# An expert layer's elementwise work taken off GpSimd, and its gathers and u tiles moved ahead of the long loop

## The chip, the cores and the metric

The kernel runs on one core of a Trainium2 chip. A core has a matrix engine (PE, with its weight loads shown as PEld), a vector engine (DVE), a scalar engine (ACT), a general engine (GpSimd, shown as POOL) and a queue engine that issues transfers (SP). Sixteen DMA engines move data between the core's memory and HBM. Every engine has its own queue and works through it in order; semaphores make it wait for others. The metric is the device time of one execution in microseconds, the median of several.

## The reference

A decoder trunk over 512 tokens of width 1024: one recurrent layer, then one attention layer, each followed by a PEER expert layer. The change touches the expert layers alone:

```python
def peer(h, w_q, sub_keys, u_tab, v_tab):
    q = (h @ w_q).reshape(B, S, PEER_HEADS, 2, PEER_HALF)          # 8 heads, 2 halves of 128
    s = jnp.einsum('bshpd,hpnd->bshpn', q, sub_keys)               # 128 keys per half
    v1, i1 = lax.top_k(s[..., 0, :], PEER_TOPK)                    # 16 best of each half
    v2, i2 = lax.top_k(s[..., 1, :], PEER_TOPK)
    cand = (v1[..., :, None] + v2[..., None, :]).reshape(B, S, PEER_HEADS, 256)
    cv, ci = lax.top_k(cand, PEER_TOPK)                            # 16 best sums
    e1 = jnp.take_along_axis(i1, ci // PEER_TOPK, axis=-1)
    e2 = jnp.take_along_axis(i2, ci % PEER_TOPK, axis=-1)
    idx = e1 * N_KEYS + e2                                         # 128 experts per token, of 16384
    g = jax.nn.softmax(cv, axis=-1)
    # per token: sum over its 128 experts of g * gelu(h . u_tab[idx]) * v_tab[idx]
```

## The kernel before

The 512 tokens are four blocks of 128. For three of them ("dense" blocks, 384 tokens) the kernel computes all 16384 experts: per tile of 128 experts it multiplies a tile of u (1024 x 128) with the hidden states, applies gelu, multiplies by a gate that is zero for experts not chosen, and multiplies with a tile of v. The fourth block gathers just its own 128 expert rows of u and of v per token by indirect DMA, 256 rows of 128 x 4 KB per layer, and DVE forms dot products (L1104) and weighted sums (L1109).

Each fp32 matrix is split into a rounded high part (ACT, `whi` or `vh`) and a rest (`wlo` or `vl`, a subtraction of 128 x 1024 at L161); a product is three matmuls (L185 to L187). A u tile (`u_part`) is thus a transfer of 512 KB, a copy, a subtraction, 24 matmuls of 384 columns and a gelu; a v tile has 18 matmuls of 512 columns. Weight buffers come in rings of three (`whi`, `wlo`) behind a ring of four raw buffers.

An expert layer goes through three stages:

- Scoring, four groups of two heads. Per group: four query tiles (`pq`, 24 matmuls of 512 columns each), scores (`sc`), top-k per block and half (L729 to L733), candidate sums on GpSimd (`candidates`), their top-k, some conditioning columns of other layers (`ada`, five a group in layer 0 and two in layer 1), and `UPQ[grp]` u tiles that keep PE busy.
- Gate. `decode` turns the top-k results of each block into expert numbers and weights; `gate_prep` transposes them. Then 24 groups of 16 tokens (`gate_group`): one-hot rows of both expert numbers (`o1`, `o2`), the first one weighted by the high and the low part of the gate (`pr[0]`, `pr[1]`), and 32 matmuls that make the tokens' gates over all experts (`wps`), stored to memory (`stg`, `wscr`, 1 MB a group). u tiles run between the groups. Block 3, the gathered one, is decoded last.
- The loop over 128 v tiles. `LEAD` u tiles are done before it (49: 8 in x, 9 in a ring of 12, 32 spilled to memory in `gscr`, 192 KB each, and read back); the other 79 run inside it, one per v tile. The gathers run here too: `goal` spreads 256 of them over the tiles by the weights `wts`.

The order on each engine is set by a scheduler from the program's order, with priorities and `issue_after` ties. In scoring and gate the u tiles' subtractions and the query tiles' are on GpSimd (`eng=nc.gpsimd`, or `wtile`'s default), as is `pr[1]` of every second half group:

```python
(nc.gpsimd if t0 else nc.vector).tensor_tensor(pr[1], o1, toks(gp[:, 1, :]), op=OP.mult)
```

## Time and profile before

| | us |
|---|---|
| median of 3 runs | 3215.36 (3213.15 to 3219.0) |
| profiled execution, its own time | 3213.07 |
| its span, first to last instruction | 3211.2 |
| mean granted clock of TensorE | 0.967 |

The profiled execution lies 2.3 us below the median, and 1.9 us of it lie around the span. Busy time is the time in which an engine executes; idle time counts only where something waits for that engine. "x" counts instructions.

### The profile page before, as it was taken

The numbers are of one execution on the slowest core, as the hardware profiler recorded it, in microseconds if no ns is written. First come the engines' busy times: TensorE is split into PE (matmuls) and PEld (weight loads), VectorE is DVE, ScalarE is ACT, GpSimd is POOL, SyncE is SP. The second block draws the span as 40 slices with busy tenths as digits, with TensorE's granted clock in tenths as the row PEclk, the third lists the DMA queues.
The fourth block names the chain that finished last, engine by engine and source line by source line (L and its number), as shares of the span: only waits on it lengthen the run. The fifth ranks groups of instructions, "written<-read, shape, count | busy, mean of one in ns | idle before, by whom it ended". The sixth has DMA issues, their size and how long they took to land. (4 is left out here: it accounts for less than half of the span.)

```text
span 3211.2 us, 43091 instructions
## 1 busy us (share of the span) xinstructions
PE 3023.7 (94%) x15334; PEld 2646.2 (82%) x15334; DVE 2631.5 (82%) x4865; ACT 1381.3 (43%) x1960; POOL 1338.0 (42%) x907
## 2 busy tenths in 40 slices
PE   6999888889999999999889989888999999999997
PEld 5658878878899999998667768888988999999996
DVE  8859999977788888888768959999766888888887
ACT  5532256643333333333456642466533333333333
POOL 0014555630244444444246625556500444444441
PEclk9999989889999999999889999999999999999999
DMA  7444445589899999999313234355698999999994
GB/s 287 147 155 154 152 152 195 178 284 319 302 355 336 346 342 332 339 335 338 117 37 101 92 128 129 113 192 182 233 311 258 339 337 331 337 334 350 337 332 161
DMA packets 319767, 786.52 MB, mean 245 GB/s; under 512 B 30784, under 2 KB 153792, under 8 KB 313152
## 3 DMA queue, kind: packets, MB, share of 16 engines
q1 hardware_dynamic: 226960, 443.61, 41.7%
q0 software_dynamic: 73728, 268.47, 23.2%
q10 hardware_dynamic: 18864, 71.69, 5.7%
q8 instruction: 121, 1.98, 0.3%
q14 instruction: 94, 0.77, 0.1%
HBM read 713.68 MB, written 69.99 MB: 244 GB/s over the span
## 5 line engine op out<-in xcount | busy, mean ns | idle before, releaser
L185 PE MATMUL u<-hh,wlo 128*128 128x384 f32 x2048 | 700.4, 342 | 10.1 <-ACT gact L896 9.7
L187 PE MATMUL u<-hh,whi 128*128 128x384 f32 x2048 | 698.8, 341 | 0.0
L186 PE MATMUL u<-hl,whi 128*128 128x384 f32 x2048 | 698.0, 341 | 0.0
L1100 POOL DMA_INDIRECT grow<-in_u_dram,idx x256 | 335.1, 1309 | 675.2 <-DVE gdot L1104 533.8
L186 PE MATMUL acc<-vl,ah 128*128 128x512 f32 x1536 | 600.8, 391 | 2.5 <-DVE vl L161 2.5
L161 POOL TENSOR_TENSOR wlo<-raw,whi 128x1024 fp32r<-128x1024 f32 (+2 forms) x183 | 401.3, 2198 | 483.4 <-ACT whi L160 470.8
L187 PE MATMUL acc<-vh,ah 128*128 128x512 f32 x1536 | 600.8, 391 | 0.0
L185 PE MATMUL acc<-vh,al 128*128 128x512 f32 x1536 | 592.1, 389 | 2.2 <-DVE al L161 2.2
L1100 POOL DMA_INDIRECT grow<-in_v_dram,idx x256 | 336.4, 1314 | 374.8 <-DVE gacc L1109 255.7
L161 DVE TENSOR_TENSOR vl<-vraw,vh 128x1024 fp32r<-128x1024 f32 x256 | 313.6, 1225 | 208.8 <-ACT vh L160 198.1
L160 ACT ACTIVATE whi<-raw 128x1024 fp32r<-128x1024 f32 (+2 forms) x364 | 350.2, 963 | 196.5 <-PE acc L187 57.8
L185 PEld LDWEIGHTS u<-hh,wlo 128*128 128x128 f32 x2048 | 393.3, 192 | 17.9 <-issue 10.2
L186 PEld LDWEIGHTS u<-hl,whi 128*128 128x128 f32 x2048 | 393.5, 192 | 6.2
L187 PEld LDWEIGHTS u<-hh,whi 128*128 128x128 f32 x2048 | 393.3, 192 | 0.0
L186 PEld LDWEIGHTS acc<-vl,ah 128*128 128x128 f32 x1536 | 288.2, 188 | 60.7 <-DVE vl L161 3.0
L187 PEld LDWEIGHTS acc<-vh,ah 128*128 128x128 f32 x1536 | 288.2, 188 | 60.3
L185 PEld LDWEIGHTS acc<-vh,al 128*128 128x128 f32 x1536 | 288.4, 188 | 59.4 <-DVE al L161 2.0
L1109 DVE SCALAR_TENSOR_TENSOR gacc<-grow,gdot,gacc 128x1024 f32<-128x1024 f32 x254 | 325.2, 1280 | 13.4 <-DMA grow<-in_v_dram,idx 12.2
L1104 DVE CUSTOM_DVE_ANT_0 grow<-grow,hn 128x1024 f32<-128x1024 f32 x256 | 308.8, 1221 | 19.0 <-DMA grow<-in_u_dram,idx 18.6
L160 ACT ACTIVATE ah<-gact 128x384 fp32r<-128x384 f32 x240 | 125.7, 524 | 438.5 <-DVE gact L985 299.1
L160 ACT ACTIVATE vh<-vraw 128x1024 fp32r<-128x1024 f32 x256 | 268.7, 1051 | 40.5 <-issue 17.7
L896 ACT ACTIVATE gact<-u 128x384 f32<-128x384 f32 x176 | 86.5, 491 | 458.4 <-PE u L187 455.0
(339 smaller groups left out, 4817.1 us busy)
## 6 DMA issues: line engine op xcount, KB each, us to landing
raw<-in_uT_dram SPq DMA_DIRECT2D x256, 512.0 KB
vraw<-in_v_dram SPq DMA_DIRECT2D x256, 512.0 KB
ada_raw<-in_adaw_dram SPq DMA_DIRECT2D x112, 512.0 KB
wscr<-stg ACTq DMA_DIRECT2D x48, 1024.0 KB
wt<-wscr SPq DMA_DIRECT2D x32, 1536.0 KB
raw<-in_w_pq_dram SPq DMA_DIRECT2D x32, 512.0 KB
gscr<-gsp ACTq DMA_DIRECT2D x64, 192.0 KB
gact<-gscr SPq DMA_DIRECT2D x64, 192.0 KB
```

What stands on the lines that cost most here:

```text
L160: nc.scalar.activation(hi, src, AF.Copy)
L161: return (eng or nc.vector).tensor_tensor(lo, src, hi.bitcast(F32), op=OP.subtract)
L185: nc.tensor.matmul(out, al, bh, start=first, stop=False)
L186: nc.tensor.matmul(out, ah, bl, start=False, stop=False)
L187: return nc.tensor.matmul(out, ah, bh, start=False, stop=last)
L896: nc.scalar.activation(gact[t], out[:, :ND], AF.Gelu)
L1100: nc.gpsimd.indirect_dma_start(out=row, out_offset=None, in_=tabs[s], in_offset=bass.IndirectOffsetOnAxis(ap=idx[:, k:k + 1], axis=0))
L1104: nc.vector.tensor_tensor_reduce(row, row, hn, op0=OP.mult, op1=OP.add, scale=1.0, scalar=0.0, accum_out=col)
L1109: nc.vector.scalar_tensor_tensor(acc, row, col, acc, op0=OP.mult, op1=OP.add)
```

## The change

All elementwise work of the expert layers leaves GpSimd for DVE. The gate's one-hot operations are merged in pairs (2048 elements instead of 1024), with the expert numbers and gates laid out by groups of eight tokens for it. The gathered block is scored first in each group, and decoded right after its scores in the last group, so its gathers can start in the gate stage: 12 steps by the end of the u tiles ahead of it, 100 by the end of the gate groups. `LEAD` rises from 49 to 93 u tiles, 76 of them spilled; 23 instead of 10 run in scoring, and those of the gate stage are tied behind the gate group two back (`after=wlast[-2]`). The weights that spread the other 156 gathers over the loop are new, and the first gates have a buffer of their own.

```diff
-SPILL = 32
+SPILL = 76
 LEAD = KC + RING - 3 + SPILL
-UPQ = (1, 2, 3, 4)
-UDEC = 6
-UEND = 3
+UPQ = (5, 6, 6, 6)
+UDEC = 9
+UEND = 5
+FIRST = 12
+EARLY = 100
...
-        nc.gpsimd.tensor_tensor(ca, v4[:, :, 0, 0:4].unsqueeze(3).to_broadcast([P, n, 4, 16]),
+        nc.vector.tensor_tensor(ca, v4[:, :, 0, 0:4].unsqueeze(3).to_broadcast([P, n, 4, 16]),
...
-            o2 = pool.tile(shp, F16, name="o2", bufs=2)
-            o1 = pool.tile(shp, F16, name="o1", bufs=2)
-            pr = [pool.tile(shp, F16, name=f"pr{q}", bufs=2) for q in range(2)]
-            nc.vector.tensor_tensor(o1, io, toks(et[:, 0, :]), op=OP.is_equal)
-            (nc.gpsimd if t0 else nc.vector).tensor_tensor(pr[1], o1, toks(gp[:, 1, :]), op=OP.mult)
-            nc.vector.tensor_tensor(o2, io, toks(et[:, 1, :]), op=OP.is_equal)
-            nc.vector.tensor_tensor(pr[0], o1, toks(gp[:, 0, :]), op=OP.mult)
+            oo = pool.tile(shp, F16, name="oo", bufs=2)
+            pr = pool.tile(shp, F16, name="pr", bufs=2)
+            nc.vector.tensor_tensor(oo, io, toks(et), op=OP.is_equal)
+            two = [P, 2, n4, P, 4]
+            nc.vector.tensor_tensor(pr.rearrange("p (q a) e t -> p q a e t", q=2), oo[:, 0:n4].unsqueeze(1).to_broadcast(two),
+                                    toks(gp).rearrange("p (q a) e t -> p q a e t", q=2), op=OP.mult)
...
-            def u_part(eng=None, after=None):
+            def u_part(after=None):
...
-                hi, lo = self.wtile(io["uT"][l][t], KC, eng=eng or nc.vector)
+                hi, lo = self.wtile(io["uT"][l][t], KC, eng=nc.vector)
...
-                            self.lin(outs[m], self.wtile(io["w_pq"][wq + m], KC), h)
+                            self.lin(outs[m], self.wtile(io["w_pq"][wq + m], KC, eng=nc.vector), h)
...
-                    for b in range(NB):
+                    for b in (nd, *range(nd)):
...
+                        if grp == 3 and b == nd:
+                            for _ in decodes((nd,)):
+                                pass
+                            gsteps = self.gather_steps(gpool, l, *gsel[0], hn)
...
                     for _ in range(UPQ[grp]):
-                        u_part(nc.gpsimd)
+                        u_part()
...
+                steps = decodes(range(nd))
+                for i in range(UDEC):
+                    u_part()
+                    while done < FIRST * (i + 1) // UDEC:
+                        next(gsteps)
+                        done += 1
...
                 for i in range(nt):
                     while state["u"] < n0 + (LEAD - UEND - n0) * (i + 1) // nt:
-                        u_part(nc.gpsimd)
-                    wlast = self.gate_group(pool, l, i // nsg, i % nsg, *prep[i // nsg])
+                        u_part(after=wlast[-2])
+                    wlast.append(self.gate_group(pool, l, i // nsg, i % nsg, *prep[i // nsg]))
...
+                    while done < min(EARLY, FIRST + (EARLY - FIRST) * (i + 1) // (nt - 2)):
+                        next(gsteps)
+                        done += 1
...
-            wts = [0.1 if t < KC + SPILL else 1.0 if t < tail else 0.5 if t < P - 2 else 0.0 for t in range(P)]
+            wts = [0.2 if t < KC else 0.6 if t < KC + SPILL else 2.6 if t < tail else 1.0 if t < P - 2 else 0.0 for t in range(P)]
```

First place: DVE in the gate stage of layer 0. Before, some ten rows between two gate tiles hold gate operations of 1024, decoding (`oh`, `rc`) and position tables (`ps_`):

```order
L834 TENSOR_TENSOR pr_4525<-o_4524,gp 128x1024
L832 TENSOR_TENSOR pr_4526<-o_4524,gp 128x1024
L833 TENSOR_TENSOR o_4523<-iota_e,et 128x1024
L798 TENSOR_TENSOR e_4589<-oh 128x64
L470 TENSOR_SCALAR ps_a<-ps_a,cst 128x512
L834 TENSOR_TENSOR pr_4553<-o_4552,gp 128x1024
L833 TENSOR_TENSOR o_4551<-iota_e,et 128x1024
L831 TENSOR_TENSOR o_4660<-iota_e,et 128x1024
L789 TENSOR_TENSOR oh<-iota_m,rc 128x1024
```

After, the same place on DVE:

```order
L835 TENSOR_TENSOR oo<-iota_e,et 128x2048
L163 TENSOR_TENSOR wlo<-raw,whi 128x1024
L798 TENSOR_TENSOR oh<-oh 128x4x64
L837 TENSOR_TENSOR pr<-oo,gp 128x2048
L1122 SCALAR_TENSOR_TENSOR gacc<-grow,gdot,gacc 128x1024
L837 TENSOR_TENSOR pr<-oo,gp 128x2048
L163 TENSOR_TENSOR wlo<-raw,whi 128x1024
L798 TENSOR_TENSOR oh<-oh 128x4x32
L1122 SCALAR_TENSOR_TENSOR gacc<-grow,gdot,gacc 128x1024
L163 TENSOR_TENSOR wlo<-raw,whi 128x1024
```

Gate operations have doubled in width and halved in number; u subtractions (`wlo`) and weighted sums of gathered rows (`gacc`) now stand between them.

Second place: DVE at the end of a scoring group of layer 0, where `ada_junk` is a conditioning column and `MAX` of `sc` begins the next group's top-k. Before:

```order
L752 MAX_INDEX ci_1544<-cv_1540,c_2146 128x8
L149 ISA ada_junk,mod<-ada_raw,csil,vecs 128x1024
L149 ISA mod 128x1
L752 MAX_INDEX ci_1544<-cv_1540,c_2152 128x8
L149 ISA ada_junk,mod<-ada_raw,csil,vecs 128x1024
L149 ISA mod 128x1
L729 MAX v_1362<-sc 128x8
```

After:

```order
L163 TENSOR_TENSOR wlo<-raw,whi 128x1024
L754 MAX_INDEX ci_1543<-cv_1539,c_2277 128x8
L754 MAX_INDEX ci_1543<-cv_1539,c_2283 128x8
L151 ISA ada_junk,mod<-ada_raw,csil,vecs 128x1024
L151 ISA mod 128x1
L151 ISA ada_junk,mod<-ada_raw,csil,vecs 128x1024
L151 ISA mod 128x1
L163 TENSOR_TENSOR wlo<-raw,whi 128x1024 x2
L731 MAX v_1365<-sc 128x8
```

The splits of the query and u tiles that PE needs for and after the next scores now stand behind this group's top-k and columns.

Third place: GpSimd in the last part of layer 0's gate stage. Before:

```order
L161 TENSOR_TENSOR wlo<-raw,whi 128x1024
L832 TENSOR_TENSOR pr_5674<-o_5672,gp 128x1024
L161 TENSOR_TENSOR wlo<-raw,whi 128x1024
L1100 DMA grow<-in_u_dram,idx 128x1024
L832 TENSOR_TENSOR pr_5772<-o_5770,gp 128x1024
L1100 DMA grow<-in_u_dram,idx 128x1024
```

After, from the first row that GpSimd has in layer 0's expert layer on:

```order
L1113 DMA grow<-in_u_dram,idx 128x1024 x16
L1113 DMA grow<-in_v_dram,idx 128x1024 x16
L1113 DMA grow<-in_u_dram,idx 128x1024 x16
L1113 DMA grow<-in_v_dram,idx 128x1024 x16
L1113 DMA grow<-in_u_dram,idx 128x1024 x16
```

Subtractions and products are gone from it; only gathers are left, in the order of before.

## Rows read from the trace of the kernel before

**Rows 1.** The page, part 1: busy us, share, instructions of each engine.

```profile
PE 3023.7 (94%) x15334; PEld 2646.2 (82%) x15334; DVE 2631.5 (82%) x4865; ACT 1381.3 (43%) x1960; POOL 1338.0 (42%) x907
```

**Rows 2.** Windows by stage: length, busy PE, PEld, DVE, ACT, POOL, clock, DMA share, GB/s.

```profile
229.00:396.00 167.00, 159.78 (x842) 144.12 (x840) 146.75 (x812) 47.22 (x63) 89.72 (x63) 0.98 0.48 152
396.00:693.00 297.00, 248.90 (x1572) 239.61 (x1573) 273.59 (x361) 173.45 (x205) 170.26 (x68) 0.87 0.54 184
693.00:1548.00 855.00, 850.62 (x4172) 757.12 (x4170) 697.90 (x898) 309.66 (x422) 335.15 (x252) 1.00 0.95 335
1905.00:2051.00 146.00, 145.21 (x783) 132.08 (x782) 126.16 (x788) 43.64 (x59) 85.08 (x61) 1.00 0.40 123
2051.00:2331.00 280.00, 252.24 (x1626) 242.14 (x1625) 249.76 (x316) 171.56 (x204) 161.61 (x69) 0.92 0.55 190
2331.00:3175.00 844.00, 844.00 (x4148) 752.86 (x4147) 668.49 (x847) 309.80 (x418) 322.14 (x252) 1.00 0.93 323
```

**Rows 3.** Waits, 396 to 693 us: us in total, times, longest.

```profile
PE wps L839 <- DVE o L833: 32.4, 14, 7.3
```

**Rows 4.** Short windows, columns as in rows 2.

```profile
318.00:328.00 10.00, 4.78 (x13) 3.60 (x12) 10.00 (x70) 1.44 (x2) 5.77 (x6) 0.75 0.44 152
700.00:800.00 100.00, 100.00 (x443) 82.78 (x442) 70.77 (x103) 36.90 (x50) 8.26 (x7) 1.00 0.98 335
860.00:880.00 20.00, 20.00 (x106) 18.51 (x105) 19.03 (x25) 7.63 (x11) 10.81 (x9) 1.00 1.03 406
2600.00:2700.00 100.00, 100.00 (x507) 91.01 (x506) 82.20 (x101) 36.45 (x49) 44.78 (x35) 1.00 0.96 340
```

**Rows 5.** The chain that ended last, gate stage of layer 1: start, us, what.

```profile
2314.82 3.77 PE wps L839 x32
```

**Rows 6.** Timeline, gate stage of layer 0: start, us, engine, line, operation.

```profile
454.56 2.77 POOL L161 TENSOR_TENSOR wlo<-raw,whi 128x1024 fp32r<-128x1024 f32 x1 [0.77 <-ACT whi L160]
455.06 2.82 DVE L833 TENSOR_TENSOR o<-iota_e,et 128x1024 f16<-128x1024 f16 x1
457.81 0.41 DVE L796 TENSOR_TENSOR oh<-oh 128x512 bf16<-128x512 bf16 x1
...
458.95 0.68 DVE L833 TENSOR_TENSOR o<-iota_e,et 128x1024 f16<-128x1024 f16 x1
459.55 0.68 DVE L831 TENSOR_TENSOR o<-iota_e,et 128x1024 f16<-128x1024 f16 x1
```

**Rows 7.** Groups by form, 396 to 693 us: count, busy us, mean ns, idle before.

```profile
L833 DVE TENSOR_TENSOR o<-iota_e,et 128x1024 f16<-128x1024 f16 x48 | 50.7, 1056 | 0.3 <-PE wps L839 0.3
L831 DVE TENSOR_TENSOR o<-iota_e,et 128x1024 f16<-128x1024 f16 x48 | 43.4, 909 | 6.5 <-POOL pr L832 6.5
L834 DVE TENSOR_TENSOR pr<-o,gp 128x1024 f16<-128x1024 f16 x48 | 40.0, 835 | 4.5 <-PE wps L839 4.4
L832 DVE TENSOR_TENSOR pr<-o,gp 128x1024 f16<-128x1024 f16 x24 | 30.2, 1258 | 0.0
L832 POOL TENSOR_TENSOR pr<-o,gp 128x1024 f16<-128x1024 f16 x24 | 62.5, 2604 | 44.2 <-DVE o L831 23.0 <-PE wps L839 12.3 <-DVE gsum L778 5.2
```

**Rows 8.** Groups by form, 1100 to 1500 us, in layer 0's loop.

```profile
L1104 DVE CUSTOM_DVE_ANT_0 grow<-grow,hn 128x1024 f32<-128x1024 f32 x78 | 94.4, 1220 | 2.6 <-DMA grow<-in_u_dram,idx 2.4
L1109 DVE SCALAR_TENSOR_TENSOR gacc<-grow,gdot,gacc 128x1024 f32<-128x1024 f32 x64 | 81.9, 1280 | 7.1 <-DMA grow<-in_v_dram,idx 6.8
L161 DVE TENSOR_TENSOR wlo<-raw,whi 128x1024 fp32r<-128x1024 f32 x48 | 58.8, 1225 | 26.0 <-ACT whi L160 25.7
L161 DVE TENSOR_TENSOR al<-gact,ah 128x384 fp32r<-128x384 f32 x49 | 27.1, 552 | 0.0
L1100 POOL DMA_INDIRECT grow<-in_u_dram,idx x77 | 101.9, 1324 | 118.1 <-DVE gdot L1104 84.9 <-DVE gacc L1109 29.9 <-issue 3.3
```

**Rows 9.** Timeline, end of the gate stage of layer 0.

```profile
652.69 5.25 POOL L1100 DMA_INDIRECT grow<-in_u_dram,idx  x1 [2.17 <-PE u L185]
652.93 0.68 DVE L834 TENSOR_TENSOR pr<-o,gp 128x1024 f16<-128x1024 f16 x1
653.53 0.68 DVE L832 TENSOR_TENSOR pr<-o,gp 128x1024 f16<-128x1024 f16 x1
```

## What I expect of the change, and why

> **What bounds the kernel now.** I read the page's first lines, then a table of windows cut at the stages of the two expert layers, then the groups inside one stage. The page alone misleads: PE 94%, DVE 82%, GpSimd 42% [rows 1] are means over unlike stages. By stage [rows 2] the picture splits. The long expert loop (693 to 1548 us in layer 0, 2331 to 3175 in layer 1) has PE busy throughout at a granted clock of 1.00, with DVE at 80% and the DMA engines at 93 to 95%: PE sets its length. The gate stage (396 to 693, 2051 to 2331) has DVE busy 274 of 297 us and 250 of 280, PE busy 84 to 90%, and the granted clock at 0.87 and 0.92, so part of the time at 1.2 GHz, the lower of its two levels. PE stands there waiting for the one-hot tiles of DVE [rows 3].
>
> Busy PE time is not PE need, since matmuls overlap, so I work out a pace. An accumulating V matmul starts every 100/443 = 0.2257 us [rows 4], so a V tile (18 of them) takes 4.06 us and 128 tiles 520 us. Layer 1's loop holds 79 u tiles besides and takes 844 us [rows 2]: (844 - 520)/79 = 4.10 us per u tile. 32 gate matmuls take 3.77 us, 0.118 each [rows 5]. What PE needs before the loop is then: 49 u tiles 201 us, 14 query tiles of 24 matmuls 76, 128 score matmuls 15 (an estimate, at the gate matmuls' pace), 768 gate matmuls 91, together 383. Scoring and gate take 167 + 297 = 464 us in layer 0 and 146 + 280 = 426 in layer 1 [rows 2]. So PE loses **81 and 43 us** there, to waits and to the lower clock, and some 11 us more in layer 0's loop (855 against 844). These 135 us are all that a better order could win.
>
> Why DVE is slow in the gate stage: two-input 16-bit operations of 128x1024 take 0.68 us and start 0.60 us apart when GpSimd is quiet; beside a GpSimd subtraction of 2.77 us the same operation takes 2.82 [rows 6]. Over the stage their means are 0.84 to 1.26 us [rows 7]: 168 of them take 164 us where 168 x 0.68 = 114 would do, and GpSimd's own products take 2.6 us each.
>
> **The change, part by part.** *GpSimd's elementwise work goes to DVE.* Per layer 49 u splits, 14 query splits, 24 gate products and the small decode and candidate operations leave GpSimd, whose queue then holds the gathers alone. On DVE a split takes 1.22 us [rows 8] and, by the 0.08 us overlap seen in [rows 6], costs a step of 1.14.
>
> *Gate operations of double width.* Four of 1024 become two of 2048. From 512 to 1024 elements the time goes from 0.41 to 0.68 us [rows 6], so 2048 is estimated at 0.68 + 2 x 0.27 = 1.22, a step of 1.14: 96 x 1.14 = 109 us per layer on DVE, against 164 + 62 on the two engines now [rows 7].
>
> *44 more u tiles ahead of the loop* (SPILL 76), their outputs through memory. They leave 35 in the loop, so the loop needs 520 + 35 x 4.10 = 664 us instead of 844 to 855; ahead of it PE needs 383 + 44 x 4.10 = 563. PE's sum does not change; only its losses can.
>
> *100 of 256 gathered rows ahead of the loop*, each costing DVE 1.14 (dot product) or 1.20 us (weighted sum) [rows 8]. DVE's need from the start of scoring to the loop in layer 0, by steps: 192 top-k instructions per group at 10/70 = 0.143 us [rows 4], 110 for four groups; candidate sums 6; 20 conditioning columns at about the dot product's 1.2 us, 24; 107 splits 122; four decodes of about 12 (estimate: 16 passes of 0.60 + 0.60 + 0.33 + 0.5 and small ones) 48; gate 109; gathers 117. That is 536 us against PE's 563; 522 in layer 1, which has 8 columns. In the loop: 128 x (1.14 + 0.47 + 0.47) + 35 x 1.14 + 156 x 1.17 = 489, with layer 0's columns and its position tables some 540, of 664. **PE becomes the bound in every stage**, by a small margin in the first ones, and the stalls behind GpSimd vanish.
>
> What is late next, per layer:
> - Scoring. Query splits now stand in DVE's queue behind the top-k work and the columns (order, second place). Per group DVE needs 29 + 6 + 10 x 1.14 = 46 us in layer 0, and idles some 6 us while PE ends the last query tile (5.4) and scores; PE needs 6 x 4.1 + 22 + 4 = 50. I take 10 us lost in layer 0 over three groups, 2 in layer 1 (DVE 42 + 6 = 48).
> - The start of the gate. From the last scores on, DVE has the last top-k group 29, columns 6, 19 splits 22, two decodes 24, 16 gathered rows 18 and two gate tiles 2 before the first product: 101 us (97 in layer 1). PE has 19 u tiles in that stretch (6 of the last group, 9, and 4 issued with the first gate groups), 78. A hole of **25 and 21 us** with the clock's recovery. Putting gathers there isn't free.
> - The gate proper. PE needs 52 u tiles and 91, 304 us; DVE, from the first product to the last, some 260. So DVE waits for PE, not the reverse. The DMA engines move per gate group 4 rows 2.10 MB, 2.2 u tiles 1.14, the gates 1.05, spilled outputs 0.43: 4.7 MB in 12.7 us, 372 GB/s. The loop shows 340 over 100 us, but 406 over 20 us with PE solid [rows 4]. Between a loss of nothing (406) and of (13.8 - 12.7) x 24 = 27 us (340) I take 8, nearer the first because the loop's 340 is what it asks for, not a ceiling.
> - The loop. V tiles 67 MB, u 18, rows 82, gates 25, spilled outputs 15, in layer 0 columns and x 15: 222 MB in 664 us, 334 GB/s, as now. I take 8 and 3 us.
>
> The Trainium skill, in "SBUF — State Buffer", section "Summary: rules for kernel authors", puts HBM transfers at about 358 GB/s; by that figure the gate loses (13.1 - 12.7) x 24 = 11 us, which is an estimate and 3 us from mine. Windows above it exist in this trace.
>
> Sum. Layer 0: 563 + 664 + 51 lost = 1278 against 464 + 855 = 1319, **-41**. Layer 1: 1227 + 34 = 1261 against 1270, **-9**. The profiled execution took 3213.07 us, 2.3 below the median of 3215.36. 3213 - 50 = 3163; beside the median **3165 us** (-1.6%). This likeliest case by itself spans 3140 to 3190, its four losses being uncertain by half.
>
> **Rivals.**
> - *The hole at the gate's start closes*, because PE is still behind with its u tiles when DVE gets there. Nothing in the rows excludes it. Both holes gone: 3165 - 46 = 3119.
> - *The DMA engines become the bound of the gate* at the loop's 340 GB/s: 19 us more per layer than I took, 3203. For it: 93 to 95% busy in the loop [rows 2]; against: 406 GB/s.
> - *The wide operations run at one element per cycle.* At that rate 384 elements take 0.55 us and 1024 take 1.22 [rows 8], so 2048 take 2.29, 1.07 us more on 96 of them: DVE 363 us against PE's 304, 59 per layer, 3283. The inner pattern is the narrow ones', which speaks against.
> - *Slower: DVE waits for gathered rows.* DVE's queue is in order; a late row now holds up gate tiles and u splits, for which PE waits with only three weight buffers. DVE's spare time in the gate is 304 - 260 = 44 us over 88 rows, 0.5 us each. The loop waits 9 us over 142 row reads, 0.07 each [rows 8]. The gain is gone when the mean wait passes 0.5 + 25/88 = 0.8 us; at 1.2 us it costs 62 per layer, 3289. For it: DMA near its limit, a ring of four rows.
> - *Gathers block DVE.* If GpSimd's descriptor work held up DVE's two-input operations as its subtractions do, 100 x 1.3 us [rows 8] less 44 spare is 86 per layer, 3337. Against it: 0.68 us operations run unslowed beside a DMA_INDIRECT of 5.25 us [rows 9], and the loop's two-input 1.22 and 1.28 us are even. The Trainium skill, in "SBUF — State Buffer", section "Who interferes with whom", has a DVE instruction with two SBUF inputs contend with a GpSimd instruction that reads SBUF; the gather reads its index there, and the trace does not bear that out.
>
> **How the numbers follow.** Chances: likeliest 0.54, hole closes 0.13, DMA bound 0.15, wide operations slow 0.04, late rows 0.12, blocked by gathers 0.02. 0.2%, or 6 us, is about what this kernel's measurement tells from nothing: faster means under 3209. Faster: 0.54 + 0.13 + two thirds of 0.15, 0.77. Same: the rest of the DMA case and a mild form of the late rows, 0.07. Slower: 0.16. The range 3112 to 3215 takes in the first three cases and leaves out the slow ones.
>
> **What would show it.** Right: gate operations of 1.2 us without long ones; GpSimd without TENSOR_TENSOR before the attention layer; a loop of about 670 us at clock 1.00; scoring and gate together near 600; PE idle 15 to 25 us before the first gate matmul, DVE busy. Wrong: DVE waits on gathered rows over 0.5 us, a loop above 690, DMA share at 1.0 in the gate with PE waiting for weights.

## The result, and the profile after

The changed kernel takes **3195.9 us** (3191.91 to 3203.43) against 3215.36: a ratio of 0.9944, 95% interval 0.9933 to 0.9955. It is faster, by 19.5 us where 50 were forecast. The profiled execution took 3191.91 us with a span of 3190.1.

The page's line of busy times, as in [rows 1]:

```profile
PE 3003.0 (94%) x15334; PEld 2633.5 (83%) x15334; DVE 2582.8 (81%) x4927; ACT 1379.5 (43%) x1960; POOL 859.8 (27%) x653
```

Windows by stage, columns as in [rows 2]; a window ends at the first gate product, the first V matmul or the end of the loop:

```profile
237.00:500.00 263.00, 231.58 (x1289) 219.23 (x1288) 246.89 (x1022) 92.90 (x121) 25.79 (x20) 0.94 0.59 189
500.00:839.00 339.00, 328.37 (x2095) 320.13 (x2094) 285.26 (x326) 180.52 (x220) 129.75 (x81) 0.98 0.92 321
839.00:1528.00 689.00, 682.55 (x3186) 588.48 (x3185) 554.52 (x753) 254.17 (x342) 201.02 (x156) 0.99 0.95 327
1882.00:2137.00 255.00, 231.01 (x1284) 218.53 (x1283) 230.02 (x995) 91.16 (x119) 22.17 (x18) 0.96 0.53 168
2137.00:2490.00 353.00, 335.43 (x2118) 326.08 (x2117) 286.87 (x327) 184.30 (x223) 129.83 (x84) 0.97 0.91 319
2490.00:3164.00 674.00, 673.98 (x3160) 582.55 (x3161) 512.34 (x659) 245.24 (x334) 182.99 (x154) 1.00 0.90 303
```

Against [rows 2] scoring and gate have grown, the loops have shrunk, as the change says. GpSimd's share falls from 42% [rows 1] to 27%; its gathers remain. The clock of gate and tail together is nearly whole (0.98 and 0.97), where the windows of [rows 2], which hold the wait before the first product too, had 0.87 and 0.92.

To find the time I cut each expert layer, in every kernel, at the same events: first and last score matmul, first and last gate product, first V matmul, first transposition of the outputs. A stretch's need is its count of matmuls times the pace, the median distance of their starts (0.2265 us for 512 columns, 0.173 for 384, that is 4.15 per u tile, 0.118 per gate product, 0.112 per score matmul); loss is its length less its need. "Hole" is last score to first gate product, "tail" last gate product to first V matmul. A few matmul records are missing, so a loss can be some tenths too high. Each row comes from one profile; e3 below, which runs as the changed kernel does, differs from it by up to 2 us in a stage. In us, layer 0 / layer 1 (the other kernels are told in the text):

| kernel | scoring | hole | gate | tail | loop | sum |
|---|---|---|---|---|---|---|
| before | 9 / 0 | 18 / 9 | 51 / 33 | 1 / 0 | 13 / 6 | 91 / 49 |
| after | 0 / 0 | 33 / 26 | 14 / 14 | 5 / 15 | 16 / 5 | 68 / 59 |
| e1_no_extra_u | 5 / 2 | 58 / 40 | 3 / 4 | 1 / 0 | 6 / 6 | 73 / 51 |
| e4_rows_in_loop | 1 / 0 | 10 / 8 | 1 / 2 | 0 / 0 | 144 / 114 | 157 / 124 |
| e5_rows_behind_vector | 0 / 0 | 10 / 8 | 20 / 21 | 2 / 5 | 37 / 8 | 69 / 42 |
| e6_rows_not_loaded | 0 / 0 | 10 / 8 | 24 / 17 | 0 / 1 | 7 / 3 | 42 / 29 |
| e7_rows_not_used | 0 / 0 | 10 / 8 | 61 / 47 | 15 / 14 | 3 / 3 | 89 / 72 |
| e8_tiles_ahead_of_gate | 3 / 0 | 21 / 15 | 37 / 34 | 1 / 1 | 6 / 6 | 68 / 57 |
| e9_copy_behind_gelu | 4 / 4 | 33 / 25 | 8 / 7 | 1 / 15 | 24 / 5 | 69 / 56 |
| e10_both_ties | 4 / 4 | 14 / 11 | 4 / 2 | 13 / 17 | 24 / 3 | 59 / 37 |
| e15_tables_early | 7 / 4 | 14 / 11 | 7 / 3 | 18 / 16 | 7 / 3 | 53 / 36 |

From first score to outputs the two layers take 1290.3 + 1281.9 us after, 1313.9 + 1270.9 before: 12.6 us gained, 24 in layer 0 and -11 in layer 1. The span shrank by 21.1; the other 8.5 lie before layer 0 (1.6) and in the attention layer (354.3 against 361.3), whose code is the same. That stretch takes 354 to 366 us in the profiles of all kernels here, so the 7 us lie within its scatter.

The hole, in the waits of PE from 388 to 500 us (layer 0): total us, times, longest.

```profile
PE et L808 <- DVE e L800: 19.1, 2, 13.0
PE wps L843 <- DVE pr L837: 12.4, 1, 12.4
```

PE waits there for DVE's decode and first gate operation, as forecast. DVE also runs the 16 early dot products in that stretch, and stands 5.2 us waiting for their rows (3.9 in layer 1):

```profile
L1117 DVE CUSTOM_DVE_ANT_0 grow<-grow,hn 128x1024 f32<-128x1024 f32 x16 | 19.4, 1215 | 5.2 <-DMA grow<-in_u_dram,idx 5.2
```

DVE's groups in the gate, by form, 500 to 813 us (count, busy us, mean ns, idle before):

```profile
L163 DVE TENSOR_TENSOR wlo<-raw,whi 128x1024 fp32r<-128x1024 f32 x50 | 61.1, 1223 | 17.0 <-ACT whi L162 15.7 <-ACT gsp L895 1.3
L837 DVE TENSOR_TENSOR pr<-oo,gp 128x2048 f16<-128x2048 f16 x47 | 56.9, 1220 | 0.0
L835 DVE TENSOR_TENSOR oo<-iota_e,et 128x2048 f16<-128x2048 f16 x46 | 56.3, 1223 | 24.7 <-PE wps L843 24.6
L1122 DVE SCALAR_TENSOR_TENSOR gacc<-grow,gdot,gacc 128x1024 f32<-128x1024 f32 x43 | 55.1, 1280 | 0.1
```

The wide operations take 1.22 us, the estimate itself, beside gathers too; against [rows 7] the stalls are gone. DVE's idle time is spent waiting for PE and ACT. So what does PE wait for? First the gate's end in layer 0 (740 to 840 us), then in layer 1 (2330 to 2500):

```profile
PE u L187 <- ACT gsp L895: 9.3, 7, 2.5
...
PE u L187 <- ACT gsp L895: 12.0, 8, 2.6
PE acc L187 <- ACT vh L162: 5.2, 1, 5.2
```

And ACT's timeline in that place (start, duration, idle before):

```profile
787.79 1.06 ACT L162 ACTIVATE whi<-raw 128x1024 fp32r<-128x1024 f32 x1 [6.31 <-PE u L189]
788.75 1.10 ACT L846 ACTIVATE stg<-wps 128x512 f32<-128x512 f32 x1
793.54 1.07 ACT L162 ACTIVATE whi<-raw 128x1024 fp32r<-128x1024 f32 x1 [3.69 <-PE u L189]
794.51 2.80 ACT L846 ACTIVATE stg<-wps 128x512 f32<-128x512 f32 x3
...
797.72 0.49 ACT L895 ACTIVATE gsp<-u 128x384 f32<-128x384 f32 x1 [0.40 <-ACT stg L846]
...
798.63 0.49 ACT L895 ACTIVATE gsp<-u 128x384 f32<-128x384 f32 x1 [0.42 <-ACT gsp L895]
```

Two weight copies stand ahead of two gelus. Each copy sits 4 to 6 us at the queue's head until PE frees a weight buffer; the gelu of a finished tile waits behind it, and PE then waits for the bank that this gelu empties. From first to last gate product PE stands idle for 6.4 and 5.9 us, all of it such waits. Most of the rest of the gates' 14 us passes right there, with PE busy but slower than its pace. In layer 0 the granted clock is 1.00 from 510 to 760 us and falls where PE has been waiting for gelus:

```profile
780.00:800.00 20.00, 16.86 (x85) 16.19 (x86) 14.05 (x13) 7.80 (x10) 5.41 (x4) 0.76 0.79 269
800.00:813.00 13.00, 13.00 (x77) 12.78 (x77) 9.20 (x9) 4.77 (x6) 4.75 (x4) 0.86 0.87 289
```

Two more places carry loss. The first is layer 1's tail (ACT's waits, 2400 to 2500 us):

```profile
ACT vh L162 <- DMA wt<-wscr: 10.3, 1, 10.3
```

This comes of the transfer ahead of the copy in ACT's queue, a spilled output whose issue stands from 2478.6 to 2488.5. The second is layer 0's loop (GpSimd's timeline):

```profile
901.48 1.56 POOL L1113 DMA_INDIRECT grow<-in_u_dram,idx  x1 [73.17 <-DMA rscr<-ps_a]
```

The gathers stop for 73 us: the position tables of the attention layer have borrowed the four row buffers (tag "grow"). Here DVE works on the tables from 848 to 917 us. In the kernel before it did so in the gate stage, just ahead of the rows; its first and last operation on them:

```profile
524.00 0.42 DVE L469 CAST ps_a<-ps_pi 128x512 f32<-128x512 int32 x1
...
654.74 0.41 DVE L514 TENSOR_SCALAR ps_mb<-ps_u 128x512 bf16<-128x512 f32 x1
```

The early rows now fill the buffers there, and the tables come behind them, in the loop. (Without early rows, in e1 and e4 below, DVE makes them in scoring, from 220 to 260 us.)

### The profile page after: what moved, and what is told of

It reads as the page before. It is cut to its first block, busy times and chain, and to the rows that moved or that the text cites. A ratio compares the mean times of both kernels' runs of the same rounds, so it can differ in the third digit from the quotient of the medians.

```text
span 3190.1 us, 43195 instructions
## 1 busy us (share of the span) xinstructions
PE 3003.0 (94%) x15334; PEld 2633.5 (83%) x15334; DVE 2582.8 (81%) x4927; ACT 1379.5 (43%) x1960; POOL 859.8 (27%) x653
## 4 chain that ended last, share of the span: by engine, by line
PE 77%; DVE 11%; DMA 4%; ACT 4%; issue 3%; POOL 1%; ACTq 0%; SPq 0%; DVEq 0%; POOLq 0%
PE acc L187 10%; PE acc L188 10%; PE acc L189 10%; PE u L187 10%; PE u L188 9%; PE u L189 9%; PE wps L843 5%; PE pq L187 2%; PE pq L189 2%; PE pq L188 2%; DVE wlo L163 1%; PE wo L207 1%; DMA grow<-in_u_dram,idx 1%; ACT stg L846 1%; DVE ada_junk L151 1%
## 5 line engine op out<-in xcount | busy, mean ns | idle before, releaser
L187 PE MATMUL acc<-vh,al 128*128 128x512 f32 x1536 | 563.5, 392 | 12.4 <-ACT vh L162 7.5
L1113 POOL DMA_INDIRECT grow<-in_v_dram,idx x256 | 350.9, 1371 | 680.0 <-DVE gacc L1122 467.9
L163 DVE TENSOR_TENSOR wlo<-raw,whi 128x1024 fp32r<-128x1024 f32 x307 | 376.8, 1227 | 112.7 <-ACT whi L162 105.8
L846 ACT ACTIVATE stg<-wps 128x512 f32<-128x512 f32 x192 | 190.9, 1094 | 70.8 <-PE wps L843 66.8
```

What stands on the lines that cost most here:

```text
L163: return (eng or nc.vector).tensor_tensor(lo, src, hi.bitcast(F32), op=OP.subtract)
L187: nc.tensor.matmul(out, al, bh, start=first, stop=False)
L846: nc.scalar.activation(stg[:, :, c:c + 4].rearrange("p e t -> p t e"), wps.rearrange("p (t e) -> p t e", t=4), AF.Copy, scale=1.0 / GSCALE)
L1113: nc.gpsimd.indirect_dma_start(out=row, out_offset=None, in_=tabs[s], in_offset=bass.IndirectOffsetOnAxis(ap=idx[:, k:k + 1], axis=0))
```

## The experiments

Each edit is against the changed kernel unless said. Times are medians with the ratio to the kernel before, whose medians in these rounds lay between 3213.7 and 3215.4 us.

**e1**: the tile counts of before, and no early rows.

```diff
-SPILL = 76
+SPILL = 32
-UPQ = (5, 6, 6, 6)
-UDEC = 9
-UEND = 5
-FIRST = 12
-EARLY = 100
+UPQ = (1, 2, 3, 4)
+UDEC = 6
+UEND = 3
+FIRST = 0
+EARLY = 0
```

> The changed kernel with 32 spilled u tiles as before (10 in scoring, 6 around the decode, 30 in the gate groups, 3 behind them) and no gathered row ahead of the loop; GpSimd without elementwise work, the wide gate operations and the gathered block first stay. Theory (PE's need decides, and the 44 moved u tiles only change where it lies): per layer 383 + 844 us of need and the losses without the crowded end of the gate, 1282 us from first scores to the end of the loop in layer 0 and 1269 in layer 1, so 3165 to 3185, not slower than the changed kernel's 3192. Rival (the moved tiles and the early rows earn the gain, by filling PE's waits in scoring and gate): 3200 to 3215, most of the gain gone.

3194.55 us, 0.9941 (0.9928 to 0.9955): the changed kernel's time to 0.1%, and between the two ranges. The forecast of what the moved tiles earn, nothing, holds; the time is 10 us over the theory's range, since the hole is larger. Windows of layer 0, up to the first product and the gate:

```profile
237.00:455.00 218.00, 158.04 (x855) 144.90 (x854) 215.95 (x991) 64.36 (x83) 4.35 (x4) 0.87 0.45 139
455.00:678.00 223.00, 221.60 (x1517) 216.57 (x1516) 163.01 (x185) 145.26 (x172) 0.00 (x0) 0.99 0.62 217
```

With GpSimd silent and no rows in it the gate runs with PE solid (before: 51 us lost). The 44 tiles and 100 rows fill 25 of 58 and 14 of 40 us of the hole and lose about as much elsewhere.

**e12** is e1 with the splits ahead of the loop back on GpSimd (`eng=nc.gpsimd`), gate operations still on DVE.

> The run without extra u tiles and early rows (3194.6 us, gate losing 3 and 4 us), with the u and query splits ahead of the loop put back on GpSimd; the wide gate operations and all gate products stay on VectorE. Theory (a GpSimd subtraction slows VectorE's two-input operations beside it, as 0.68 us became 2.82): the wide operations' mean rises from 1.22 to over 1.8 us, the gates lose 25 to 50 us each, 3230 to 3290. Rival (only the gate products on GpSimd mattered, since the wide operations do the same work in half the instructions): the means stay under 1.4 us and the time at 3188 to 3205.

3208.27 us, 0.9981 (0.9972 to 0.9990), 14 us over e1, between the two ranges. Groups, 430 to 665 us:

```profile
L835 DVE TENSOR_TENSOR oo<-iota_e,et 128x2048 f16<-128x2048 f16 x45 | 78.6, 1763 | 40.5 <-PE wps L843 40.3
...
L163 POOL TENSOR_TENSOR wlo<-raw,whi 128x1024 fp32r<-128x1024 f32 x29 | 73.5, 2540 | 151.0 <-ACT whi L162 151.0
L837 DVE TENSOR_TENSOR pr<-oo,gp 128x2048 f16<-128x2048 f16 x44 | 52.3, 1215 | 0.0
```

The mean of one wide operation rises to 1.76 us, that of the other does not. Over the whole run, the 28 of 96 `oo` operations that overlap a GpSimd subtraction take 2.96 us on average and the others 1.22, while the 9 `pr` operations that overlap one take 1.22. The gate hides it (4 and 5 us lost). It is layer 0's scoring that pays: 26 us lost in place of 5. The Trainium skill, in "SBUF — State Buffer", section "Who interferes with whom", lets a DVE instruction with two SBUF inputs contend with a GpSimd instruction that reads SBUF; both forms have two such inputs, and only the `oo` form bears it out here. So the splits' move off GpSimd is worth about two thirds of e1's gain over the kernel before. In the gate they cost nothing by themselves: that its loss falls from 51 and 33 us comes of the rest of the change (products moved, operations merged, the fourth block decoded earlier), which no run takes apart, and the hole has grown meanwhile from 18 and 9 to 49 and 37.

**e4**: `FIRST = EARLY = 0` alone.

> All 256 gathered rows of a layer stay in the expert loop, where 274 MB then have to move in 664 us, 413 GB/s. Theory (the loop's 327 to 340 GB/s are what it asked for, and windows above 400 GB/s exist): the loop takes 690 to 710 us against 690 and 674, the two holes shrink by 20 us each, and the time is 3160 to 3200. Rival (some 340 GB/s is what the DMA engines can move over hundreds of us): the loop takes 780 to 810 us, and the time is 3330 to 3400.

3351.21 us, 1.0435 (1.0415 to 1.0454): the rival's range, but not its mechanism. Windows of layer 0's gate, then of its loop in three parts, and the beginning of layer 1's loop:

```profile
478.00:807.00 329.00, 328.88 (x2140) 323.98 (x2140) 195.68 (x212) 182.26 (x225) 0.00 (x0) 0.99 0.60 204
807.00:1100.00 293.00, 277.48 (x1192) 225.62 (x1190) 238.99 (x338) 96.55 (x132) 77.66 (x65) 0.98 1.02 363
1100.00:1493.00 393.00, 390.90 (x1902) 347.35 (x1903) 327.83 (x423) 142.06 (x194) 175.08 (x131) 0.99 0.96 337
1493.00:1602.00 109.00, 4.25 (x19) 3.19 (x17) 73.93 (x89) 3.61 (x5) 66.63 (x57) 0.54 0.84 285
...
2544.00:2844.00 300.00, 300.00 (x1326) 248.43 (x1325) 249.37 (x335) 109.50 (x151) 73.48 (x72) 1.00 1.00 355
```

Most of the 144 and 114 us that the loops lose is one wait in each (PE's waits, 807 to 1616 and 2545 to 3331 us):

```profile
PE acc L187 <- ACT vh L162: 122.6, 8, 106.5
...
PE acc L187 <- ACT vh L162: 106.4, 1, 106.4
```

In the program the last two V tiles (`LAST`) are split into the row buffers, tag "grow". When PE reaches them 57 rows are still to be gathered, and PE stands until nearly all are through, with the DMA engines at a share of 0.84. Before that the engines carry 363 GB/s over 293 us, at a share of 1.02 with PE idle for 15, and 355 over 300 us with PE solid. The averages over the two whole loops, 337 and 325 GB/s, are thus not a ceiling. What the early rows buy is that the rest is through when the V tiles are. What holds the rows back until then (four buffers, DVE's order, or a DMA share of 0.96) isn't shown; more row buffers weren't tried. In the gate, without rows, 1 and 2 us are lost, in the tail nothing: all that the changed kernel loses there comes with the rows.

**e2**: `with tc.high_priority():` around the spilled gelu.

> The gelu of a spilled u tile is given priority in the order of ScalarE's queue, so that it stands ahead of the next weight tile's copy and no longer behind two of them. Theory (at the end of the gate two copies stand ahead of two gelus; the copies wait for PE's u matmuls, and PE then waits for a bank that the gelus have yet to empty): the waits of PE u on ACT gsp, 9.3 us in layer 0 and 12.0 in layer 1, fall under 3 each, and the time to 3167 to 3180. Rival (the end of the gate is bound by its DMA transfers): the waits of PE move to weight tiles or rows and the time stays within 3187 to 3196.

3198.62 us, 0.9952 (0.9939 to 0.9966). ACT's order at the end of the gate came out as it was, pairs and all, with 9.3 us of the same wait: the edit did not make the test.

**e3**: `FIRST = 0`, and the early rows under `tc.issue_after(wlast[-1])`.

> No gathered row ahead of the first gate product: the rows before the loop are tied each to the product ahead of it. Theory (the hole before the first product is as long as DVE's queue, in which the 16 early dot products take 19.4 us and wait 5.2 for their rows): the hole of 29 and 22 us shrinks to under 12 and 6, and since DVE has some 43 us to spare in the gate, the time falls to 3145 to 3165. Rival (DVE's spare time in the gate is not to be had, since its operations wait for PE and PE for them in turn): the hole shrinks and the gate grows by as much, 3185 to 3196.

3198.97 us, 0.9943 (0.9930 to 0.9957). The tie names a PE instruction and orders PE's queue alone; 16 dot products still ran ahead of the first product. The run repeats the changed kernel: its hole is 33 and 27 us, and its time shows how far such repeats lie apart, 3 us.

**e5**: the same tie, to DVE's operation, with `FIRST = 0`.

```diff
-            nc.vector.tensor_tensor(pr.rearrange("p (q a) e t -> p q a e t", q=2), oo[:, 0:n4].unsqueeze(1).to_broadcast(two),
-                                    toks(gp).rearrange("p (q a) e t -> p q a e t", q=2), op=OP.mult)
+            self.last_pr = nc.vector.tensor_tensor(pr.rearrange("p (q a) e t -> p q a e t", q=2), oo[:, 0:n4].unsqueeze(1).to_broadcast(two),
+                                    toks(gp).rearrange("p (q a) e t -> p q a e t", q=2), op=OP.mult).ins
...
+                    with tc.issue_after(self.last_pr):
```

> As the run before that tied the gathered rows to the product, but tied to VectorE's own operation (that run's tie was to TensorE's product, which does not order VectorE's queue, and 16 dot products stayed ahead of the first product). Now no dot product stands ahead of the first gate product in VectorE's queue. Theory (the hole is VectorE's queue): PE loses 11 and 8 us instead of 33 and 26 up to the first product, as the run without early rows did; the gate, with 16 rows more, loses 5 to 15 more than 19 and 29; time 3160 to 3180. Rival (the gate gives all of it back, because its transfers are the bound): 3187 to 3200.

3185.45 us, 0.9907 (0.9893 to 0.9922), short of the theory's range. The hole shrinks as forecast, from 33 and 26 us to 10 and 8. Gate and tail together keep their loss (22 and 26 us for 19 and 29), with more of it in the gate. Half of the hole's gain is lost again in the loops, 21 us in layer 0's.

**e6, e7**: e5 with the first 100 rows not loaded (DVE works on `hn` in their place), and e5 with them loaded but DVE's work on them cut to one column. In e6:

```diff
+                    early = 2 * k0 + s * n + k - k0 < EARLY
+                    if not early:
...
-                        nc.vector.tensor_tensor_reduce(row, row, hn, op0=OP.mult, op1=OP.add, scale=1.0, scalar=0.0,
+                        nc.vector.tensor_tensor_reduce(row, hn if early else row, hn, op0=OP.mult, op1=OP.add, scale=1.0, scalar=0.0,
```

> As the run before (rows tied behind VectorE's gate operation), but the first 100 rows of each layer are not loaded: their dot products and weighted sums read a tile that is there, at the same cost to VectorE. Theory A (the gate's loss of 19 and 29 us is the DMA engines' load of rows): the gate loses under 8 in each layer, the time is 40 to 60 us below the run with the loads. Theory B (it is VectorE's work on the rows, which delays weight splits and gate operations): the loss stays, and the time is within 15 us of the run with the loads.

> The converse: the first 100 rows of each layer are loaded as before, but VectorE's dot products and weighted sums on them read one column in place of 1024. Theory A (the DMA engines' load): the gate still loses 15 to 30 us in each layer. Theory B (VectorE's work on the rows): it loses under 8, and the time is 40 to 60 us below the run that uses the rows.

3142.0 us (0.9768, 0.9755 to 0.9781) and 3231.59 (1.0052, 1.0038 to 1.0066). e6's time is in theory A's range, but its gates lose as much as with the loads (24 and 17); the 43 us come from tail, loops (37 to 7 in layer 0) and layer 1's gate. The gates' loss is of another kind, though. e5 has 9.3 and 10.2 us of waits for gelus there, e6 none; in e6's layer 0 (477 to 808 us) PE waits for gate operations instead:

```profile
PE wps L843 <- DVE pr L837: 26.6, 4, 10.0
```

So e6 doesn't settle what the loads cost the gate. Without DVE's work (e7) the gate loses two to three times as much, so theory B falls, and the loss lies above theory A's range too. e7's waits of 477 to 882 us name a third:

```profile
ACT whi L162 <- PE u L189: 146.4, 40, 7.0
...
PE u L187 <- ACT gsp L895: 32.7, 16, 5.2
```

It is the copy at the head of ACT's queue, in 40 places.

**e8**: `SPILL = 32`, `UEND = 3`, `FIRST = EARLY = 0`.

> The changed kernel's 23 u tiles in scoring and 9 around the decode, but 32 spilled tiles as before the change (14 in the gate groups, 3 behind them) and no early rows. From the runs so far: the run without early rows lost 11 and 8 us up to the first product with these 32 tiles, and under 3 in the gate; the run with 32 spilled tiles lost 6 us in each loop, at 337 and 318 GB/s. Theory (what costs is rows and u tiles in the gate, what earns is u tiles ahead of it; the losses add): 1223 + 11 + 4 + 7 and 1223 + 8 + 4 + 6 us, 1245 and 1241, against 1291 and 1282: 3090 to 3120. Rival (with 17 u tiles behind the first product VectorE, at 109 + 19 + 24 us, is slower than PE's 161 there): the gate loses 20 us or more in each layer, 3135 to 3160.

3198.45 us, 0.9943 (0.9930 to 0.9955): both times missed, though the gates lose over 20 us as the rival said (37 and 34). With one u tile for about every second gate group PE and DVE wait for each other (478 to 660 us, all engines' waits):

```profile
DVE oo L835 <- PE wps L843: 36.3, 24, 3.7
...
PE wps L843 <- DVE pr L837: 27.8, 11, 4.0
```

`oo` and `pr` have two buffers. In e4, with the changed kernel's u tiles between the groups, the same buffers lose 1 and 2 us.

**e9**: the copy of a u tile queued behind the gelu of the tile two before it; **e10**: e9 with e5's tie.

```diff
-                hi, lo = self.wtile(io["uT"][l][t], KC, eng=nc.vector)
+                with tc.issue_after(gel[-2]) if 2 <= t < LEAD else ExitStack():
+                    hi, lo = self.wtile(io["uT"][l][t], KC, eng=nc.vector)
```

> The changed kernel with one tie more: on ScalarE, the copy of a u tile's weights is queued behind the gelu of the u tile two before it. In the changed kernel's queue, from the middle of the gate on, two copies stand ahead of two gelus; the run that gave the gelus priority left that order as it was there. Theory (a copy waits for PE to free a weight buffer, the gelus wait behind it, and PE waits for the bank that they empty): the waits of PE u on ACT gsp, 9.3 and 12.0 us, fall under 3 each, gate and tail lose under 10 and 15 us in place of 19 and 29, and the time is 3160 to 3178. Rival (VectorE's work on the rows, or their load, is what the gate loses, and the waits move to weight tiles or gate operations): gate and tail lose as much as before, 3187 to 3198.

> The tie of copies behind gelus and the tie of the rows behind VectorE's gate operation together. Theory (two separate losses, which add): first product with 10 and 8 us lost, gate and tail under 15 in each layer, 3145 to 3168. Rival (VectorE is the bound of the gate once the 16 rows are in it): gate and tail lose 22 to 30 us as in the run with the rows' tie alone, 3178 to 3190.

e9 takes 3190.3 us (0.9927, 0.9914 to 0.9941), e10 **3167.71** (0.9856, 0.9841 to 0.9871). In e9 PE's wait for the gelu is gone. What is left at the gate's end (750 to 840 us), and the longest wait in layer 1 (2350 to 2500), in the tail:

```profile
PE u L187 <- DVE wlo L163: 0.6, 1, 0.6
...
PE acc L187 <- ACT vh L162: 10.4, 1, 10.4
```

The mechanism is shown: the gates lose 8 and 7 us in place of 14 and 14. Yet only 6 us arrive, a time in the rival's range: layer 1's tail keeps its 15 us, scoring loses 4 more per layer, layer 0's loop 8.

e10 differs from e5 by the copies' tie alone, and its gates lose 4 and 2 us in place of 20 and 21, with the same 100 rows. The time just reaches the theory's range, but the parts don't all: the holes lose 14 and 11 us, and gate and tail 17 and 19, over the 15 forecast, since the tails lose 11 and 12 more than in e5. e5 gave 10 us, e9 6, both 28. Singly, e5 loses part of its gain in layer 0's loop and e9 in scoring and that loop; why the two together lose less there than their sum (24 us in layer 0's loop, where e5 alone loses 37) wasn't taken apart.

**e11**: e10 with `EARLY = (100, 76)` and loop weights 0.5, 2.6, 1.8 in place of 0.6, 2.6, 1.0.

> Both ties; 76 early rows in place of 100 in layer 1, whose loop moves 303 GB/s and has room for 24 rows more (322); and in both loops fewer rows among the spilled tiles and more at the end, where the DMA share was 0.85. Theory (the loop loses where its DMA share passes 1.0, 355 to 371 GB/s in 900 to 1100 us, and the gate where VectorE has too much): layer 1's gate loses 10 us less and layer 0's loop 5 to 10 less than with both ties alone, 3130 to 3155. Rival (the loops are full: 24 rows more cost layer 1 as much as the gate gains): within 6 us of the run with both ties.

3165.88 us, 0.9843 (0.9830 to 0.9856), as the rival said: layer 1's tail loses 5 in place of 17 us, its loop 14 in place of 3.

**e13, e14**: e10 with the last 8 spilled outputs not written (`if t < LEAD - 8`), or written from GpSimd's queue (and e11's loop weights).

> Both ties, and the last 8 spilled u tiles of a layer are not written to memory (the loop reads an earlier tile in their place; 1.6 MB less, 5 us at 340 GB/s). Theory (ScalarE stands 15 us at the issue of such a write until the load of the gates has landed, and the weight copies and gelus queued behind it stop PE): the waits of ACT gsp on DMA wt, 15.1 and 15.5 us, go, the tails lose under 6 us each in place of 13 and 17, and the time is 3142 to 3156. Rival (the DMA engines are full there, share 1.00 to 1.04, and weights come late whoever issues): the tails lose 9 us or more, 3158 to 3168.

> Both ties, the writes of the last 8 spilled u tiles issued by GpSimd in place of ScalarE, and in the loops fewer rows among the spilled tiles and more at the end. Theory (ScalarE's issue is what blocks): the tails lose under 8 us each, 3143 to 3160. Rival (GpSimd's queue holds the writes up behind gathers that wait for row buffers, up to 13 us each, and the gelus run out of their two buffers): the tails lose 13 us or more, 3165 to 3185.

3166.25 us (0.9856, 0.9841 to 0.9871) and 3163.92 (0.9849, 0.9835 to 0.9862). e13's waits for the gates' load are gone, and its tails still lose 9 and 10 us, layer 0's loop 33. Its two tails in windows:

```profile
783.00:825.00 42.00, 35.46 (x190) 34.73 (x190) 23.63 (x26) 13.42 (x21) 12.64 (x10) 0.92 1.00 323
2407.00:2466.00 59.00, 52.42 (x292) 51.41 (x292) 39.49 (x45) 21.42 (x31) 24.88 (x18) 0.94 1.03 365
```

The DMA share is at 1.0 there. In e14 ACT is free of the writes too, and waits for u weights to land instead (780 to 835 us); its tails lose 18 and 17:

```profile
ACT whi L162 <- DMA raw<-in_uT_dram: 15.8, 1, 15.8
```

The blocked issue is real, and mending it earns nothing in the time: e13's tails lose 4 and 6 us less, with 1.6 MB less to move as well, and layer 0's loop 9 more.

**e15, e16**: `self.positions(gpool)` moved from V tile 2 to the second scoring group of layer 0, in e10 and in the changed kernel.

```diff
+                    if l == 0 and grp == 1:
+                        self.positions(gpool)
                     for _ in range(UPQ[grp]):
...
-                if l == 0 and t == 2:
-                    self.positions(gpool)
```

> Both ties, and the position tables computed in layer 0's scoring in place of its expert loop. Theory (in the loop they hold the four row buffers for 75 us, and the rows that were stopped come in a burst that crowds out V tiles): layer 0's loop loses under 10 us in place of 24, scoring at most 8 more, and the time is 3145 to 3160 against 3167.7. Rival (layer 0's loop is short of DMA throughput with or without the stop): the loop loses 18 us or more, 3162 to 3176.

> The changed kernel with the position tables in layer 0's scoring alone. Theory (as for the run with both ties): layer 0's loop loses under 8 us in place of 16; 3178 to 3190. Rival: 3188 to 3202, the loss stays or VectorE pays it in scoring.

**3158.62 us** (0.9827, 0.9813 to 0.9840) and 3187.3 (0.9918, 0.9905 to 0.9932): the theory in both. Layer 0's loop loses 7 in place of 24, and 3 in place of 16. Windows of e15's loop:

```profile
900.00:1000.00 100.00, 98.11 (x431) 80.62 (x431) 79.71 (x112) 36.41 (x49) 23.05 (x16) 1.00 1.00 350
1000.00:1100.00 100.00, 100.00 (x442) 82.83 (x442) 81.82 (x119) 37.77 (x50) 18.12 (x16) 1.00 1.02 356
```

With 16 rows in each the engines carry 350 to 356 GB/s and PE is busy for 98 and 100 us. In e5, whose 1000 to 1100 us hold 26 rows, PE lost 18 us. The move takes the tables' work off DVE's queue in the loop along with their hold on the buffers, so the two aren't separated; the stop of 73 us and the crowd of rows behind it speak for the buffers. e15 is the fastest version that gathers all its rows, 1.2% under the changed kernel.

## Why the prediction was wrong

**What held.** PE is the bound in gate and loop, and DVE in the hole; GpSimd's stalls vanish; the wide operations take 1.22 us; in the gate DVE does not wait for rows (0.6 us before the 32 dot products of layer 0's gate). "PE's sum does not change; only its losses can" holds most plainly in e1.

**The step that failed is the losses after**, 51 and 34 us in the sum, 68 and 59 measured; those of before were 92 and 43, measured 91 and 49. Term by term:

- Scoring, 10 and 2: nothing was lost.
- The hole, 25 and 21: 33 and 26. The mechanism was right and the size low: DVE's stretch took 112 and 105 us where 101 and 97 were summed. The 16 rows in it, priced at 18, took 24.6 in layer 0, 5.2 of them waiting. e5 shows that these rows are worth 23 and 18 us of the hole.
- The gate, 8 each, with the tail: 19 and 29. This is the main miss, 32 us. I priced a queue of transfers, and ACT's queue was not in the sum. e9 and e10 show the gate's part to be the order of copies and gelus there: with the order mended the same rows and bytes lose 4 and 2 us (e10) in place of 20 and 21 (e5). In the changed kernel half of the gate's 14 us is those waits, and most of the rest the lower clock behind them (0.76 from 780 to 800 us); the sum had the clock's recovery in the hole alone. The tail's part comes with the loads of rows, since it is 0 to 1 us in e4 and e6, and falls where the DMA share is at 1.0; the sum had the DMA engines only as an average over the gate.
- The loop, 8 and 3: 16 and 5. I counted the position tables as DVE work and did not see that the early rows push them out of the gate stage into the loop, where they hold the four row buffers. e16 shows that moving them away leaves 3 us of the 16; that it is the buffers and not DVE's work on them is argued.

**The rival that came nearest in time**, the DMA engines as the bound of the gate at 340 GB/s (3203), did so by luck. From first gate product to first V matmul the engines moved 321 and 319 GB/s at a share of 0.92 and 0.91, the gates' waits were for gelus, and e10 moves the same rows there with 4 and 2 us lost in the gates. Full DMA engines go with PE's losses in shorter stretches: the tails, 900 to 1100 us of layer 0's loop, and the first 300 us of it in e4. My reading that "the loop's 340 is what it asks for, not a ceiling" is borne out by e4's 363 GB/s over 293 us.

**What stays open** is the tail, 13 to 18 us in e10 and e15. Two loads of gates of 1.5 MB fall there beside rows and weights; whether they could start elsewhere wasn't tried. The hole's last 14 and 11 us in e10 were not taken apart, nor what limits the rows in e4's loop.

## What to carry to other kernels

Moving work ahead of a loop buys nothing where the bound engine's need stays the same: count its losses stage by stage, before and after, and go through every in-order queue for what a waiting instruction holds up, the engine with 43% busy time included. Where several stalls are in line, mending one passes its gain on to the next, so judge a mend by its own wait and try mends together before dropping one. When work is started earlier, look for borrowed buffers that it now finds taken.

## What the runs showed of the hardware

- Throughput depends on the stretch: in e4's loops 363 GB/s over 293 us (share 1.02) and 355 over 300 us (share 1.00), and 285 over the 109 us in which hardly anything but gathers was left (share 0.84). The Trainium skill, in "HBM Reference", section "Specifications (TRN2)", has a core that streams alone reach about 425 GB/s, with its DMA engines as the bound. No stretch of 40 us or more in the windows shown here comes near that, though PE stood waiting in some of them.
- A transfer can hold up the engine that issues it. ACT stood 10.3 us at the issue of a 192 KB write until an unrelated 1.5 MB load had landed (15.5 in e10); the write's list of waits in the program names one of eight semaphores that all such transfers share in turn.
- Gathers leave DVE alone: in the gate, 75 of them beside DVE's work, the wide operations keep 1.22 us, while GpSimd subtractions take one form to 2.96 where they overlap it (e12) and leave the other at 1.22.
